# The last block of an MLP: partial sums loaded by plain transfers and added by VectorE

## The chip, the cores and the metric

One Trainium2 chip; the program runs on one of its cores. The metric is the device time of one execution in microseconds (us), as the median of several executions. The engines are called by the profile's names: PE (TensorE matmul) with its weight loads PEld, DVE (VectorE), ACT (ScalarE), POOL (GpSimd) and SP (SyncE). POOL and SP hardly compute here; they issue DMA transfers, POOL on queue q0, SP on queue q1. Both queues are served by the same 16 DMA engines.

## The reference

A decoder of two layers on 256 tokens of width 2048, in float32. Each layer is an attention mixer, an MLP and a gated embedding; the two mixers differ, the two MLPs don't. What matters here is the MLP:

```python
D_MODEL, SEQ, DEPTH = 2048, 256, 2
D_FF = 4 * D_MODEL
...
    for i in range(DEPTH):
        ...                                       # mixer A (i = 0) or mixer B (i = 1)
        hn = rmsnorm(h, mlp_norm_g[i])
        h = h + jnp.square(jax.nn.relu(hn @ mlp_w1[i])) @ mlp_w2[i]
        gate = jax.nn.sigmoid(rmsnorm(h, ple_norm_g[i]) @ ple_w_gate[i])
        h = h + (p[i] @ ple_w_proj[i]) * gate
    return rmsnorm(h, final_norm_g)
```

## The kernel before, in words

**Products.** A float32 product is made of three matmuls: each operand is split into a rounded part and a rest. A weight chunk is 128x1024 (512 KB). SP loads it into `raw` (L240, 5 buffers), ACT writes its rounded part `whi` (L252, 6 buffers), DVE the rest `wlo` (L260, 5 buffers); PE multiplies by both. An ordinary chunk is twelve matmuls, four of them with `wlo`. `Program.run` writes out the order of all this: when it emits the matmuls of a chunk it has emitted the splits of the three chunks behind it, and every generator that is under way (an epilogue, a fetch) goes on by one `yield` a chunk. There is no scheduler beyond that: each engine runs its instructions in the order in which they were emitted, and waits for semaphores. An instruction that waits on DVE therefore holds up every `wlo` behind it.

**The MLP** (`mlp`, L738). The hidden width of 8192 goes in four blocks b = 0 to 3 of 2048; each block has four column quarters q of 512, in w1 (up) and in w2 (down). The down results of all blocks have to be summed: for b < 3, `down_kept` (L902) puts each quarter's result through POOL into the DRAM tiles `y[q]`, with an adding transfer where b > 0 (`keep_sum`, L846). The last block adds those sums to its own results, turns each 128x1024 row tile to the layout of the residual x (`turned`, L698: DVE transposes it, one transfer takes it to DRAM, four bring it back) and adds it to x (`add_turned`, L726).

**Pairs of quarters.** Quarters 0 and 1 of a down block are made together (`pair_major`, L470). For some chunks it makes seven products in place of eight (a scheme of Strassen's kind), four of them into PSUM banks of their own: P1, R6, Q5, Q7. These are kept apart, summed over the blocks in DRAM as `shared[q]` (two tiles, in the profile `s`), and only at the end combined by four 128x512 operations of DVE (`from_sums`, L881, operations L882 to L885) and added to both quarters. In blocks 0 to 2 quarters 2 and 3 are a pair too; in the last block they are made one after the other by `downs`, and need the kept sums `shared[2]` and `y[2]`, `y[3]` alone.

**The last block, b = 3.** Around `down_mixed(3, 0)`, the pair (0, 1), 18 chunks, numbered 0 to 17 here, and then two times eight chunks of `downs(3, 2)` and `downs(3, 3)`:

- `down_last` (L920). After the chunks of the four extra products, ACT copies P1 and R6 into one row tile and Q5 and Q7 into another (L928), POOL adds the kept `shared[0]` to each by an adding transfer (L930), DVE combines (`from_sums`), POOL adds `y[0]` and `y[1]` by adding transfers (L936). Then `done` adds the pair's own banks, quarter 0 after chunk 15 and quarter 1 after chunk 17 (L945), and starts the turning.
- `fetch(2)` (L887), begun after chunk 14: POOL loads `shared[2]` into two row tiles (L890), DVE combines, POOL adds `y[2]`, `y[3]` (L896). `down` uses these tiles (L856).
- Ahead of all this the last two up quarters of the block pass through POOL: `dU<-z`, four `w<-dU` and four `y<-dU` (L206, L210), each ending in a tile `h` that ACT and DVE split (L778, L780). The first `h` is read from chunk 10 on, the second from chunk 14 on.

Row tiles have the tag `y` (4 buffers, L976). The tag `xf` has four 128x1024 tiles: sums of activations that the up products of the pairs read (`x_forms`, L557); after the last `up_mixed` of a layer nothing reads them.

Of the kernel before, what the change touches and what calls it, by code (L numbers as in the profile page):

```python
# [11 lines left out]
F32R = mybir.dt.float32r  # L12
AF = mybir.ActivationFunctionType
ALU = mybir.AluOpType

P = 128
D = 2048
T = 256
# [10 lines left out]
NFB = 4  # L29
# [8 lines left out]
MIXED = (2, 3, 5, 6)  # L38
# [10 lines left out]
def mixed_down(b, q):  # L49
    return (0, 4) if (b, q) not in ((0, 0), (NFB - 1, 0)) else (0,)  # L50


def f32(ap):
    return ap.bitcast(F32)
# [116 lines left out]
def kernel(ctx: ExitStack, tc: tile.TileContext, a: dict, out: bass.AP):  # L171
    nc = tc.nc
# [12 lines left out]
    cur = {}  # L185
# [535 lines left out]
    def add_turned(q, w):  # L721

        for n in range(2):
            xn = xp[2 * q + n].rearrange("p (f a r) -> p f a r", a=4, r=32)
            wn = w.rearrange("p a (f r) -> p f a r", r=32)[:, 4 * n:4 * n + 4]
            nc.vector.tensor_add(xn, wn, xn)  # L726

    def in_pairs(make, q):

        for n in (0, 2):  # L730
            gs = [make(4 * q + n + i) for i in range(2)]
            for g in gs:
                next(g)
            yield
            for g in gs:
                next(g, None)

    def mlp(layer, xg, norm, to, norm2, opening):  # L738
# [6 lines left out]
        y = [dpool.tile([P, D // 2], F32, tag=f"y{q}", name=f"y{q}", bufs=1) for q in range(4)]  # L745
        shared = {q: [dpool.tile([P, D // 2], F32, tag=f"s{q}{i}", name=f"s{q}{i}", bufs=1) for i in range(2)] for q in (0, 2)}
        hid = [[None] * 16 for _ in range(NFB)]
        forms = [None] * (KT // 2)
        sums_so_far = {}
# [5 lines left out]
        def row():  # L755
            return row_tile()
# [118 lines left out]
        def all_forms(these):  # L875
            for c in these:
                yield from x_forms(2 * c, G_MLP + layer, forms)
                yield
        taken_late(lambda: ups(0, 0, {4: [lambda: norm.factor(rows=True)]}), lambda: ups(0, 1), opening,
                   [lambda: all_forms(MIXED[:3])])  # L880
        def from_sums(r, o):  # L881
            nc.vector.tensor_sub(r[:, 1], r[:, 1], r[:, 0])  # L882
            nc.vector.tensor_add(o[:, 0], o[:, 0], r[:, 1])
            nc.vector.tensor_sub(r[:, 1], o[:, 1], r[:, 1])
            nc.vector.tensor_sub(o[:, 1], o[:, 0], o[:, 1])  # L885

        def fetch(q):  # L887
            rows = row(), row()
            for i in range(2):
                nc.gpsimd.dma_start(flat(rows[i]), shared[q][i])  # L890
            for _ in range(4):
                yield
            from_sums(*rows)
            yield
            for i in range(2):
                nc.gpsimd.dma_start(flat(rows[i]), y[q + i], accum_op=ALU.add)  # L896
                sums_so_far[q + i] = rows[i]

        def turning_tile(n):
            return f32(cur["z"].tile([P, 2, 2 * T], F32R, tag="hf", name="hf", bufs=2).rearrange("p c n -> p (c n)"))  # L900
# [20 lines left out]
        def down_last(q):  # L921
            ts = []

            def sums(aux):
                rows = row(), row()
                for t, names, kept in zip(rows, (("P1", "R6"), ("Q5", "Q7")), shared[q]):
                    for j, n in enumerate(names):
                        nc.scalar.copy(t[:, j], aux[n])  # L928
                    yield
                    nc.gpsimd.dma_start(flat(t), kept, accum_op=ALU.add)  # L930
                for _ in range(4):
                    yield
                from_sums(*rows)
                yield
                for i in range(2):
                    nc.gpsimd.dma_start(flat(rows[i]), y[q + i], accum_op=ALU.add)  # L936
                for _ in range(2):
                    yield
                ts.extend(rows)

            def done(i, ps):
                while not ts:
                    yield
                t = ts[i]
                nc.vector.tensor_add(t, ps, t)  # L945
                yield
                w = yield from turned(t, turning_tile if i else new, steps=3)
                add_turned(q + i, w)
                yield
                yield from in_pairs(normed, q + i)  # L950

            return sums, done

        def down_mixed(b, q):
            sums, done = down_kept(b, q) if b < NFB - 1 else down_last(q)
            m = mixed_down(b, q)
            if (b, q) == (0, 0):
                order = [(i, c) for i in range(2) for c in (1, 2, 3)] + [(0,)] + [(i, c) for c in (4, 5) for i in range(2)]
            else:
                order = [(0, c) for c in (1, 2, 3)] + [(0,)] + [(1, c) for c in (1, 2, 3)]  # L960
                order += [(0, 5), (1, 5), (4,)] if len(m) == 2 else [(i, c) for c in (4, 5) for i in range(2)]
            order += [(i, c) for i in range(2) for c in (6, 7)]
            pair_major(lambda i, c: a["w2"][layer * 128 + (b * 4 + q + i) * 8 + c], order, hid[b], turned_forms[b], sums, done,
                       {(0, 0): {13: [lambda: all_forms(MIXED[3:])]}, (NFB - 1, 0): {14: [lambda: fetch(2)]}}.get((b, q)), (3, 1, 0, 2))

        up_mixed(0, 2)
        for b in range(NFB):
# [11 lines left out]
    def flat(t):  # L979
        return t.rearrange("p j c -> p (j c)")  # L980

    def row_tile():

        return cur["h"].tile([P, 2, 512], F32, tag="y", name="y", bufs=4)
# [1017 lines left out]
```

## Time and profile before

| | |
|---|---|
| runs | 2425.81, 2426.03, 2428.92 us; median 2426.03 us |
| profiled execution | 2427.97 us; its span from first to last instruction 2426.2 us |
| granted TensorE clock over the span | 0.998 |
| PE, PEld busy | 99%, 83% of the span |
| DVE, ACT, POOL busy | 82%, 61%, 6% of the span |
| HBM | 504.39 MB read, 59.24 MB written |

The times are of whole executions, the rows of the profile of one of them; 1.8 us lie around its span. The MLP's last block stands twice in the trace, in layer 0 at about 1060 to 1150 us and in layer 1 at about 2225 to 2315 us. In a timeline row the columns are the start, the duration, the engine, the line, the operation with its tiles, how many were merged, and in brackets the idle time of the engine ahead of it with what ended it. A busy PE is not PE at its peak, but an idle gap of PE is time that the program waits.

### The profile page before, as it was taken

Reading aid. Unit: us, or ns where it says so; the run is one execution under the profiler, and the core shown is the slowest. Engines: PE = TensorE matmul, PEld = TensorE weight load, DVE = VectorE, ACT = ScalarE, POOL = GpSimd, SP = SyncE. Lnnn points to the kernel's source line nnn. Section 1 sums busy time; section 2 is a strip of 40 time slices with the busy share of each in tenths; the row PEclk is TensorE's granted clock in tenths of the full one; section 3 lists DMA queues with packets and bytes.
Section 4 is the critical chain, followed back from the end, with each engine's and each line's share of the span. In section 5 each row is a group of like instructions: output and inputs, shape, how many; then the busy total and the mean of one; then the engine's idle time right before and its main releaser. Section 6 shows DMA issues by size and latency. Waiting matters only on the chain.

```text
span 2426.2 us, 33519 instructions
## 1 busy us (share of the span) xinstructions
PE 2405.9 (99%) x11613; PEld 2023.3 (83%) x11613; DVE 1987.6 (82%) x2960; ACT 1480.0 (61%) x2161; POOL 147.6 (6%) x246
## 2 busy tenths in 40 slices
PE   9999999999999999999999999999999999999998
PEld 8888888888888888887788889988888888888787
DVE  7867687688898988886777989867898898888676
ACT  6544444567566666664664788756666666666456
POOL 0000000001001100111000000000100100111000
PEclk9999999999999999999999999999999999999999
DMA  8666666778778788879886753476777878888985
GB/s 282 204 216 213 199 208 193 223 216 270 245 248 260 247 255 258 249 250 284 257 247 209 256 176 120 131 226 218 254 239 260 260 252 252 258 246 259 286 254 151
DMA packets 171882, 565.85 MB, mean 233 GB/s; under 512 B 20608, under 2 KB 36416, under 8 KB 171712
## 3 DMA queue, kind: packets, MB, share of 16 engines
q1 hardware_dynamic: 150672, 494.73, 63.4%
q0 software_dynamic: 20464, 68.19, 11.0%
q8 instruction: 91, 1.49, 0.3%
q10 hardware_dynamic: 576, 0.79, 0.1%
q14 instruction: 79, 0.65, 0.1%
HBM read 504.39 MB, written 59.24 MB: 232 GB/s over the span
## 4 chain that ended last, share of the span: by engine, by line
PE 90%; issue 4%; DMA 4%; DVE 1%; POOL 0%; ACT 0%; SPq 0%; ACTq 0%; DVEq 0%; POOLq 0%
PE at L502 33%; PE at L598 13%; PE mm L393 11%; PE mm L598 11%; PE mm L502 8%; PE mm L395 6%; PE at L393 1%; DMA dU<-z 1%; DMA y<-s 1%; DMA raw<-in_w 1%; PE at L395 1%; DVE wlo L260 1%; PE at L1824 1%; DMA w<-dU 0%; PE mm L1848 0%
## 5 line engine op out<-in xcount | busy, mean ns | idle before, releaser
L260 DVE TENSOR_TENSOR wlo<-raw,whi 128x1024 fp32r<-128x1024 f32 (+1 forms) x953 | 1094.9, 1171 | 252.7 <-ACT whi L252 85.0
L252 ACT CAST whi<-raw 128x1024 fp32r<-128x1024 f32 (+1 forms) x953 | 939.2, 1013 | 451.8 <-DMA raw<-in_w 133.4
L502 PE MATMUL at<-whi,h 128*128 128x512 f32 x1504 | 463.3, 389 | 0.4 <-DVE h L780 0.4
L393 PE MATMUL mm<-xa,whi 128*128 128x512 f32 x1104 | 372.4, 396 | 0.0
L502 PE MATMUL at<-whi,xa 128*128 128x512 f32 x1144 | 352.1, 389 | 0.0
L502 PEld LDWEIGHTS at<-whi,h 128*128 128x128 f32 x1504 | 282.3, 188 | 59.5 <-DVE h L780 0.8
L502 PE MATMUL at<-wlo,h 128*128 128x512 f32 x752 | 292.7, 389 | 0.4 <-DVE wlo L260 0.4
L395 PE MATMUL mm<-xa,wlo 128*128 128x256 f32 x1104 | 274.2, 278 | 0.0
L502 PEld LDWEIGHTS at<-whi,xa 128*128 128x128 f32 x1144 | 214.7, 188 | 44.5
L502 PE MATMUL at<-wlo,xa 128*128 128x512 f32 x572 | 222.5, 389 | 0.0
L395 PEld LDWEIGHTS mm<-xa,wlo 128*128 128x128 f32 x1104 | 207.3, 188 | 17.7
L393 PEld LDWEIGHTS mm<-xa,whi 128*128 128x128 f32 x1104 | 193.5, 188 | 31.0 <-issue 0.4
L598 PE MATMUL at<-whi,xa 128*128 128x512 f32 x672 | 208.1, 391 | 0.1
L598 PE MATMUL mm<-whi,xa 128*128 128x512 f32 x656 | 202.7, 390 | 0.0
L502 PEld LDWEIGHTS at<-wlo,h 128*128 128x128 f32 x752 | 141.1, 188 | 30.0 <-DVE wlo L260 0.8
L252 ACT CAST whi<-ts 128x1024 fp32r<-128x1024 f32 x78 | 82.0, 1051 | 123.0 <-DVE ts L540 122.1
L598 PEld LDWEIGHTS at<-whi,xa 128*128 128x128 f32 x672 | 124.8, 188 | 26.3 <-ACT whi L252 0.8
L598 PEld LDWEIGHTS mm<-whi,xa 128*128 128x128 f32 x656 | 122.5, 188 | 25.0
L598 PE MATMUL at<-wlo,xa 128*128 128x512 f32 x336 | 130.9, 391 | 0.2 <-DVE wlo L260 0.2
L598 PE MATMUL mm<-wlo,xa 128*128 128x512 f32 x328 | 127.7, 389 | 0.0
L502 PEld LDWEIGHTS at<-wlo,xa 128*128 128x128 f32 x572 | 107.4, 188 | 22.4
L260 DVE TENSOR_TENSOR wlo<-ts,whi 128x1024 fp32r<-128x1024 f32 x78 | 95.1, 1220 | 8.8 <-PE at L502 4.5
(445 smaller groups left out, 3377.9 us busy)
## 6 DMA issues: line engine op xcount, KB each, us to landing
raw<-in_w SPq DMA_DIRECT2D x512, 512.0 KB, 5.2
raw<-in_w_qk SPq DMA_DIRECT2D x96, 512.0 KB, 4.2
raw<-in_w_gate SPq DMA_DIRECT2D x64, 512.0 KB, 4.8
raw<-in_w_kv SPq DMA_DIRECT2D x48, 512.0 KB, 4.4
raw<-in_w_v SPq DMA_DIRECT2D x47, 512.0 KB, 4.5
y<-y POOLq DMA_DIRECT2D x32, 512.0 KB, 9.2
raw<-in_w_q SPq DMA_DIRECT2D x32, 512.0 KB, 4.4
raw<-in_w_oB SPq DMA_DIRECT2D x32, 512.0 KB, 3.7
```

What stands on the lines that cost most here:

```text
L252: nc.scalar.copy(hi[:, c], t[:, c])
L260: nc.vector.tensor_sub(lo[:, c], t[:, c], f32(hi)[:, c])
L393: nc.tensor.matmul(ps, hi[:, col:col + P], rhs, start=first, stop=False)
L395: nc.tensor.matmul(ps[:, :T], lo[:, col:col + P], rhs[:, :T], start=False, stop=last)
L502: nc.tensor.matmul(ps, x_, w_, start=b not in touched, stop=end and last[b] == n and i == 2)
L598: nc.tensor.matmul(st[j], *parts[j][i], start=k == i == 0, stop=k == kt - 1 and i == 2)
L1824: nc.tensor.transpose(tr[:, i * P:(i + 1) * P], src, ident)
```

## The change

Nothing adds by transfer in the last block any more. `fetch_shared(q)` loads the two kept product sums `shared[q]` by plain transfers into two `xf` tiles, `fetch(q)` loads `y[q]` into a row tile. `down_last` lets DVE add the PSUM banks to the loaded tiles (four adds of 128x512, in place of ACT's four copies), then `from_sums`, then DVE adds the row tiles (`with_y`, 128x1024 each). `finish_sums(2)` does the same for quarters 2 and 3, with two more adds. The loads are hooks: `shared[0]` after chunk 1, `y[0]` and `y[1]` after chunk 6, `shared[2]` after chunk 12, `y[2]` and `y[3]` after chunk 14.

```diff
--- before.py
+++ after.py
@@ -884,17 +884,31 @@
             nc.vector.tensor_sub(r[:, 1], o[:, 1], r[:, 1])
             nc.vector.tensor_sub(o[:, 1], o[:, 0], o[:, 1])
 
+        kept = {}
+
+        def fetch_shared(q):
+
+            kept[q] = [cur["z"].tile([P, 2, 2 * T], F32R, tag="xf", name="xf", bufs=len(MIXED)) for _ in range(2)]
+            kept[q] = [f32(t) for t in kept[q]]
+            for i in range(2):
+                nc.gpsimd.dma_start(kept[q][i], shared[q][i])
+
         def fetch(q):
-            rows = row(), row()
+            sums_so_far[q] = row()
+            nc.gpsimd.dma_start(flat(sums_so_far[q]), y[q])
+
+        def with_y(q, i):
+            nc.vector.tensor_add(kept[q][i], kept[q][i], sums_so_far[q + i])
+            sums_so_far[q + i] = kept[q][i]
+
+        def finish_sums(q):
+            for _ in range(6):
+                yield
+            from_sums(*kept[q])
             for i in range(2):
-                nc.gpsimd.dma_start(flat(rows[i]), shared[q][i])
-            for _ in range(4):
-                yield
-            from_sums(*rows)
-            yield
-            for i in range(2):
-                nc.gpsimd.dma_start(flat(rows[i]), y[q + i], accum_op=ALU.add)
-                sums_so_far[q + i] = rows[i]
+                for _ in range(2):
+                    yield
+                with_y(q, i)
 
         def turning_tile(n):
             return f32(cur["z"].tile([P, 2, 2 * T], F32R, tag="hf", name="hf", bufs=2).rearrange("p c n -> p (c n)"))
@@ -922,21 +936,17 @@
             ts = []
 
             def sums(aux):
-                rows = row(), row()
-                for t, names, kept in zip(rows, (("P1", "R6"), ("Q5", "Q7")), shared[q]):
+                for _ in range(3):
+                    yield
+                for t, names in zip(kept[q], (("P1", "R6"), ("Q5", "Q7"))):
                     for j, n in enumerate(names):
-                        nc.scalar.copy(t[:, j], aux[n])
+                        nc.vector.tensor_add(t[:, j], aux[n], t[:, j])
                     yield
-                    nc.gpsimd.dma_start(flat(t), kept, accum_op=ALU.add)
-                for _ in range(4):
+                from_sums(*kept[q])
+                for i in range(2):
                     yield
-                from_sums(*rows)
-                yield
-                for i in range(2):
-                    nc.gpsimd.dma_start(flat(rows[i]), y[q + i], accum_op=ALU.add)
-                for _ in range(2):
-                    yield
-                ts.extend(rows)
+                    with_y(q, i)
+                ts.extend(kept[q])
 
             def done(i, ps):
                 while not ts:
@@ -961,7 +971,9 @@
                 order += [(0, 5), (1, 5), (4,)] if len(m) == 2 else [(i, c) for c in (4, 5) for i in range(2)]
             order += [(i, c) for i in range(2) for c in (6, 7)]
             pair_major(lambda i, c: a["w2"][layer * 128 + (b * 4 + q + i) * 8 + c], order, hid[b], turned_forms[b], sums, done,
-                       {(0, 0): {13: [lambda: all_forms(MIXED[3:])]}, (NFB - 1, 0): {14: [lambda: fetch(2)]}}.get((b, q)), (3, 1, 0, 2))
+                       {(0, 0): {13: [lambda: all_forms(MIXED[3:])]}, (NFB - 1, 0): {1: [lambda: fetch_shared(0)], 6: [lambda: fetch(0), lambda: fetch(1)],
+                                         12: [lambda: fetch_shared(2)],
+                                         14: [lambda: fetch(2), lambda: fetch(3), lambda: finish_sums(2)]}}.get((b, q)), (3, 1, 0, 2))
 
         up_mixed(0, 2)
         for b in range(NFB):
```

PE has the same instructions in the same order. ACT loses the four copies. On DVE and POOL the order is another; layer 1 is shown, layer 0 has the same.

POOL before, from the turning of the last two up quarters to the end of the block (`s00`, `s01`, `s20`, `s21` are the kept products, `y0` to `y3` at the right of an arrow the kept results):

```order
L206 DMA dU_20578<-z_20557 128x1024
L210 DMA w_20577<-dU_20578 32x4x256 x4
L206 DMA dU_20664<-z_20645 128x1024
L210 DMA y_20663<-dU_20664 32x4x256 x4
L930 DMA y_20709<-s00_109 128x1024
L930 DMA y_20710<-s01_110 128x1024
L936 DMA y_20709<-y0_105 128x1024
L936 DMA y_20710<-y1_106 128x1024
L890 DMA y_20864<-s20_111 128x1024
L890 DMA y_20865<-s21_112 128x1024
L896 DMA y_20864<-y2_107 128x1024
L896 DMA y_20865<-y3_108 128x1024
```

POOL now, the same stretch:

```order
L206 DMA dU_20586<-z_20565 128x1024
L894 DMA xf_20625<-s00_109 128x1024
L894 DMA xf_20626<-s01_110 128x1024
L210 DMA w_20585<-dU_20586 32x4x256 x4
L206 DMA dU_20676<-z_20657 128x1024
L210 DMA y_20675<-dU_20676 32x4x256 x4
L898 DMA y_20714<-y0_105 128x1024
L898 DMA y_20716<-y1_106 128x1024
L894 DMA xf_20838<-s20_111 128x1024
L894 DMA xf_20839<-s21_112 128x1024
L898 DMA y_20880<-y2_107 128x1024
L898 DMA y_20882<-y3_108 128x1024
```

There are eight transfers of 512 KB as before; two of them have moved ahead of `w<-dU`, and none of the eight waits for a result of `from_sums` any more (before, the rows of L936 and L896 did).

DVE before, between the two splits of `h` and the first combination (`mm` and `at` are PSUM banks):

```order
L780 TENSOR_TENSOR h<-w,h 128x4x8x32
L260 TENSOR_TENSOR wlo<-raw,whi 128x1024 x5
L780 TENSOR_TENSOR h<-y,h 128x4x8x32
L260 TENSOR_TENSOR wlo<-raw,whi 128x1024
L882 TENSOR_TENSOR y<-y 128x512
L883 TENSOR_TENSOR y<-y 128x512
L884 TENSOR_TENSOR y<-y 128x512
L885 TENSOR_TENSOR y<-y 128x512
L260 TENSOR_TENSOR wlo<-raw,whi 128x1024 x3
L945 TENSOR_TENSOR y<-at,y 128x1024
```

DVE now, the same place:

```order
L943 TENSOR_TENSOR xf<-mm,xf 128x512 x2
L260 TENSOR_TENSOR wlo<-raw,whi 128x1024
L780 TENSOR_TENSOR h<-y,h 128x4x8x32
L882 TENSOR_TENSOR xf<-xf 128x512
L883 TENSOR_TENSOR xf<-xf 128x512
L884 TENSOR_TENSOR xf<-xf 128x512
L885 TENSOR_TENSOR xf<-xf 128x512
L260 TENSOR_TENSOR wlo<-raw,whi 128x1024
L901 TENSOR_TENSOR xf<-xf,y 128x1024
L260 TENSOR_TENSOR wlo<-raw,whi 128x1024
L901 TENSOR_TENSOR xf<-xf,y 128x1024
L260 TENSOR_TENSOR wlo<-raw,whi 128x1024 x2
```

The operations of L943 and L901 are new: four of the one (the first two stand a split ahead of these rows) and two of the other come before quarter 0's own sum, which was L945, is L955 now and stands right behind these rows. The combination stands one split earlier.

DVE before, from the turning of quarter 0 to that of quarter 1:

```order
L709 STREAM_TRANSPOSE z<-y 128x2x4x4x32
L260 TENSOR_TENSOR wlo<-raw,whi 128x1024
L882 TENSOR_TENSOR y<-y 128x512
L883 TENSOR_TENSOR y<-y 128x512
L884 TENSOR_TENSOR y<-y 128x512
L885 TENSOR_TENSOR y<-y 128x512
L945 TENSOR_TENSOR y<-at,y 128x1024
L260 TENSOR_TENSOR wlo<-raw,whi 128x1024
L709 STREAM_TRANSPOSE hf<-y 128x2x4x4x32
```

DVE now, the same stretch and what follows it:

```order
L709 STREAM_TRANSPOSE z<-xf 128x2x4x4x32
L260 TENSOR_TENSOR wlo<-raw,whi 128x1024
L955 TENSOR_TENSOR xf<-at,xf 128x1024
L260 TENSOR_TENSOR wlo<-raw,whi 128x1024
L709 STREAM_TRANSPOSE hf<-xf 128x2x4x4x32
L260 TENSOR_TENSOR wlo<-raw,whi 128x1024
L882 TENSOR_TENSOR xf<-xf 128x512
L883 TENSOR_TENSOR xf<-xf 128x512
L884 TENSOR_TENSOR xf<-xf 128x512
L885 TENSOR_TENSOR xf<-xf 128x512
L260 TENSOR_TENSOR wlo<-raw,whi 128x1024 x2
L901 TENSOR_TENSOR xf<-xf,y 128x1024
```

The combination for quarters 2 and 3 has moved behind quarter 1's sum and its turning, with two splits between.

## The prediction

> **What bounds the kernel now.** I read the page first, then the idle gaps of PE in both last blocks, then what stood ahead of the late instruction on its engine, then the transfers.
>
> ```profile
> PE 2405.9 (99%) x11613; PEld 2023.3 (83%) x11613; DVE 1987.6 (82%) x2960; ACT 1480.0 (61%) x2161; POOL 147.6 (6%) x246
> ```
>
> PE is busy for 2405.9 us of the span of 2426.2 us. Nothing can be won from its work, which the change leaves alone; what can be won is idle time of PE. The timeline of PE has these gaps in the two last blocks, and no others:
>
> ```profile
> 1113.37 0.61 PE L598 MATMUL mm<-whi,h 128*128 128x512 f32 x2
> 1116.72 0.50 PE L598 MATMUL mm<-wlo,h 128*128 128x512 f32 x1 [2.73 <-DVE wlo L260]
> ...
> 1140.03 0.50 PE L598 MATMUL at<-wlo,h 128*128 128x512 f32 x1 [1.21 <-DVE wlo L260]
> ...
> 1143.75 0.50 PE L598 MATMUL at<-wlo,h 128*128 128x512 f32 x1 [0.70 <-DVE wlo L260]
> ...
> 1183.88 0.61 PE L298 MATMUL mm<-ones,acc 128*128 128x1 f32 x4 [1.93 <-DVE acc L289]
> ...
> 2277.38 0.61 PE L598 MATMUL mm<-whi,h 128*128 128x512 f32 x2
> 2281.24 0.50 PE L598 MATMUL mm<-wlo,h 128*128 128x512 f32 x1 [3.25 <-DVE wlo L260]
> ...
> 2282.29 1.05 PE L598 MATMUL mm<-whi,h 128*128 128x512 f32 x2
> ```
>
> The two large ones, 2.73 us in layer 0 and 3.25 us in layer 1, stand at the same place, the fifth chunk of `downs(3, 2)`, and end with a late `wlo`. Behind the second, two matmuls take 1.05 us in place of 0.61 us. Why that `wlo` is late shows in DVE's timeline, layer 1:
>
> ```profile
> 2254.65 0.68 DVE L882 TENSOR_TENSOR y<-y 128x512 f32<-128x512 f32 x1
> 2258.16 0.69 DVE L883 TENSOR_TENSOR y<-y 128x512 f32<-128x512 f32 x1 [2.82 <-DMA y<-s]
> ...
> 2260.22 3.49 DVE L260 TENSOR_TENSOR wlo<-raw,whi 128x1024 fp32r<-128x1024 f32 x3
> 2265.39 1.23 DVE L945 TENSOR_TENSOR y<-at,y 128x1024 f32<-128x1024 f32 x1 [1.69 <-DMA y<-y]
> ...
> 2272.95 0.69 DVE L882 TENSOR_TENSOR y<-y 128x512 f32<-128x512 f32 x1 [2.94 <-DMA y<-s]
> 2276.78 0.69 DVE L883 TENSOR_TENSOR y<-y 128x512 f32<-128x512 f32 x1 [3.13 <-DMA y<-s]
> ...
> 2278.84 1.22 DVE L945 TENSOR_TENSOR y<-at,y 128x1024 f32<-128x1024 f32 x1
> 2279.97 1.21 DVE L260 TENSOR_TENSOR wlo<-raw,whi 128x1024 fp32r<-128x1024 f32 x1
> ```
>
> DVE waits four times for POOL's transfers, 2.82 + 1.69 + 2.94 + 3.13 = 10.6 us, all ahead of the `wlo` at 2279.97. The waits of DVE in layer 0, from 1080 to 1120 us, are the same ones:
>
> ```profile
> DVE y L883 <- DMA y<-s: 5.1, 2, 3.2
> ...
> DVE y L882 <- DMA y<-s: 2.0, 1, 2.0
> DVE y L945 <- DMA y<-y: 1.6, 1, 1.6
> ```
>
> Together 8.7 us. The loads come late because they stand in a chain, as POOL's timeline shows:
>
> ```profile
> 2243.33 0.99 POOL L930 DMA_DIRECT2D y<-s  x1
> 2245.19 0.89 POOL L930 DMA_DIRECT2D y<-s  x1 [0.86 <-ACT y L928]
> 2259.87 1.74 POOL L936 DMA_DIRECT2D y<-y  x2 [13.79 <-DVE y L884]
> 2261.13 1.58 POOL L890 DMA_DIRECT2D y<-s  x2
> 2278.49 1.80 POOL L896 DMA_DIRECT2D y<-y  x2 [15.79 <-DVE y L884]
> ```
>
> Adding transfer, DVE, adding transfer: POOL waits 13.79 and 15.79 us for `from_sums`, and `s20`, `s21` (L890), which need nothing but a place, queue behind the first wait.
>
> **The change part by part.** DVE's waits go. The kept `s00`, `s01` now go out right behind the first `dU<-z`, long before DVE adds to them; `y0`, `y1`, `s20`, `s21` and `y2` follow `y<-dU` without waiting for `from_sums`. What DVE gets for it, per layer: four adds from PSUM and four of 128x1024, and ACT loses four copies.
>
> ```profile
> L812 DVE TENSOR_TENSOR y<-mm,y x14: 682/683/686, 554.9 to 2216.3; 128x512 f32<-128x512 f32 x14
> ...
> L928 ACT COPY y<-mm x8: 577/584/592, 1077.5 to 2244.3; 128x512 f32<-128x512 f32 x8
> ```
>
> An add from PSUM is 0.68 us (L812 has the same shape), one of 128x1024 is 1.22 us (L945 above): 4 x 0.68 + 4 x 1.22 = 7.6 us more on DVE, 4 x 0.58 = 2.3 us less on ACT, which is not late here and gets no credit. Ahead of the late `wlo` stand only the four small adds and two of the large, 2.7 + 2.4 = 5.2 us, while the second `from_sums`, 4 x 0.69 = 2.8 us, moves behind it. So, even with no add hidden, that `wlo` comes 10.6 + 2.8 - 5.2 = 8.2 us earlier in layer 1 and 8.7 + 2.8 - 5.2 = 6.3 us in layer 0. PE needs 3.25 and 2.73 us of that. **Both gaps go, with 4.9 and 3.6 us to spare: 3.25 + 2.73 = 6.0 us.** What is late next is the chunk's `raw`, which waits for the buffer that `wlo` frees and so moves with it.
>
> The gaps of 1.21 and 0.70 us in layer 0 come from DVE too. It is held up just ahead of them by the turned quarter 1:
>
> ```profile
> 1136.35 1.29 DVE L726 TENSOR_TENSOR x<-hf,x 128x512 f32<-128x512 f32 x2 [1.18 <-DMA hf<-dU]
> ```
>
> That quarter's turning begins some 6 us earlier (the `wlo` behind its sum does), PE only 2.7 us. The gaps shrink by up to 1.9 us; none is possible if the loads then collide with the turning. Layer 1, with the same code, has no such gap, so I take 1.4 us. The gap of 1.93 us ends the MLP: the norm of the last quarter, whose turning waits behind the earlier ones on DVE. Between 0 and 1.9 us I take 1.0 us, the middle, since layer 1 has no gap there.
>
> The clock. These are four rows of busy time by stage (columns: length, PE, PEld, DVE, ACT, POOL, granted clock, share of the DMA engines, GB/s):
>
> ```profile
> 1060.00:1080.00 20.00, 19.61 (x86) 15.79 (x86) 18.04 (x17) 13.45 (x17) 5.04 (x10) 1.00 0.75 250
> 1080.00:1100.00 20.00, 20.00 (x90) 16.53 (x89) 11.97 (x12) 11.19 (x13) 4.85 (x7) 1.00 0.94 269
> ...
> 2240.00:2260.00 20.00, 20.00 (x90) 16.57 (x89) 11.64 (x12) 9.72 (x11) 4.19 (x7) 1.00 1.01 312
> ...
> 2280.00:2300.00 20.00, 18.76 (x76) 15.33 (x77) 14.19 (x18) 8.30 (x14) 0.29 (x1) 0.91 1.03 285
> ```
>
> Behind the gap of 3.25 us the clock is 0.91 over 20 us, which costs 0.09 x 20 = 1.8 us; behind that of 2.73 us none is lost. The loss goes with the gap. The profiled execution, 2427.97 us, is 1.94 us over the median of 2426.03 us, about this loss; I take it that the median execution lacks it and credit it against the profiled one alone. [...]
>
> The loads' price. Queue totals of the page, and the landing of the loads from POOL:
>
> ```profile
> q1 hardware_dynamic: 150672, 494.73, 63.4%
> q0 software_dynamic: 20464, 68.19, 11.0%
> ...
> y<-s POOLq DMA_DIRECT2D x8, 512.0 KB, 12.3
> ```
>
> On q1, where all is plain, 63.4% of 2426.2 us for 494.73 MB is 3.11 us a MB, 1.63 us of all engines for 512 KB. On q0 it is 266.9 us for 68.19 MB, 55 us more than at that price; over its 44 adding transfers (32 of the earlier blocks, 12 here) that is up to 1.25 us each, an estimate. Six of the eight loads of a layer lose it, 7.5 us of DMA time where the share is 0.94 to 1.03. That gets no credit of its own, but is why I expect `raw` no later.
>
> What may cost: `s00` and `s01`, 2 x 1.63 = 3.3 us, now run ahead of `w<-dU`, and so of the second `h`.
>
> ```profile
> 1089.42 1.23 DVE L780 TENSOR_TENSOR h<-y,h 128x1024 fp32r<-128x1024 f32 x1 [3.20 <-ACT h L778]
> ...
> 1091.61 0.61 PE L502 MATMUL at<-whi,h 128*128 128x512 f32 x2
> ...
> 2251.81 1.23 DVE L780 TENSOR_TENSOR h<-y,h 128x1024 fp32r<-128x1024 f32 x1 [0.20 <-ACT h L778]
> ...
> 2255.61 0.62 PE L502 MATMUL at<-whi,h 128*128 128x512 f32 x2
> ```
>
> The PE rows are the starts of chunk 14, the first to read that `h`. Ready at 1090.65 and 2253.04, it has 0.96 and 2.57 us to spare. Bounds: no wait, or 3.3 us less the spare, 2.3 + 0.7 = 3.0 us. The loads fall in a stretch with a DMA share of 0.75, 5 us free of 20, so nearer to none: 0.5 us, in layer 0.
>
> **Sum.** 3.25 + 2.73 + 1.4 + 1.0 - 0.5 = 7.9 us; with the clock 9.7 us against the profiled execution, 2427.97 - 9.7 = 2418.3 us; against the median 2426.03 - 7.9 = 2418.1 us. I predict 2418.2 us.
>
> **The rivals.**
>
> *The burst starves `raw`* (no change). Five loads queue at once on q0, where two did: 5 x 1.63 = 8.2 us of all engines. If q0 and q1 take turns, that lasts 16.3 us, in which q1 gets 8.2 us, five chunks. PE's pace is in the chain:
>
> ```profile
> 2293.58 21.76 PE at L598 x96
> ```
>
> Eight chunks in 21.76 us, 2.72 us each, six in 16.3 us. One chunk late, 2.7 us, is less than the 3.6 us to spare; with the turnings on top two may be, 5.4 us. Then PE waits 1.8 and 0.5 us again and the smaller gaps stay: 7.9 - 2.3 - 2.4 = 3.2 us won, 2422.8 us. For it: the share of 1.01. Against: the 7.5 us of DMA time that fall away. [...]
>
> *DVE becomes the bound.* 7.6 us of adds against 8.7 to 10.6 us of waits: if what is left goes into the turnings, the smaller gaps stay and only the large ones go, 6.0 - 0.5 = 5.5 us, 2420.5 us. Against: DVE is busy for 11.97 and 11.64 of 20 us there.
>
> *The turned `h` is late* (slower). If `w<-dU`, the second `dU<-z` and `y<-dU`, each behind the other, all lose the 3.3 us of the two loads, the second `h` is 9.8 us late; PE waits 8.8 and 7.2 us at chunk 14 and loses the clock twice, 1.8 us each: 19.6 - 7.9 = 11.7 us slower, 2437.7 us. It decides from d with (d - 0.96) + (d - 2.57) + 3.6 = 7.9, 3.9 us of delay. Against: only `w<-dU` is directly behind the loads.
>
> *Nothing starts earlier* (no change): POOL held at an `xf` tile that PE still reads, 2426 us. Against: `xf` is read by up products alone, and POOL's order has the loads behind the turning of those products' results.
>
> **How the numbers follow.** Forecast 0.70; DVE as the bound 0.09; starved `raw` 0.13; late `h` 0.05; nothing earlier 0.03. The low end has all gaps whole, 2.73 + 1.91 + 1.93 + 3.25 = 9.8 us, and the clock in the median too, 1.8 us: 2414.4, say 2414.2 us. The high end takes in starved `raw`: 2423.0 us. 0.2%, about what a measurement can tell, is 4.9 us, so faster means under 2421.2 us: 0.68 of the forecast and 0.07 of DVE's case, 0.75; slower 0.05; the rest 0.20.
>
> **What would show it.** Right: no wait of DVE for a transfer ahead of `from_sums` or the quarters' sums; no gap of PE at the fifth chunk of `downs(3, 2)`; a clock of 1.00 there; POOL's loads with no wait for DVE, but for `y3`, whose place the second `h` frees. Wrong: a gap of PE ahead of `at<-whi,h` at chunk 14 (late `h`), ACT waiting for `raw` with PE idle (the burst), or `wlo` late with DVE busy all along.

## The result, and the profile after

| | before | after |
|---|---|---|
| median of the runs | 2425.98 us (2425.81 to 2428.92, 4 runs) | 2414.42 us (2414.18 to 2414.48, 4 runs) |
| profiled execution, span | 2427.97, 2426.2 us | 2414.44, 2412.7 us |

The ratio is 0.9949, 95% interval 0.9932 to 0.9967: 11.6 us faster by the medians, where 7.8 us were predicted. The range began at 2414.2 us: the median is just inside it, and by the ratio, 0.9949 x 2426.03 = 2413.7 us, the time is just below. PE's work is the same 11613 matmuls; the page of the changed kernel has

```profile
PE 2402.0 (100%) x11613; PEld 2023.0 (84%) x11613; DVE 2001.4 (83%) x2976; ACT 1477.6 (61%) x2153; POOL 142.6 (6%) x246
...
q1 hardware_dynamic: 150672, 494.73, 63.9%
q0 software_dynamic: 20464, 68.19, 10.5%
```

Packets and MB of both queues are the same as before; q0 takes 253.3 us of all 16 engines in place of 266.9 (share times span), 13.6 us less for twelve transfers that no longer add, 1.1 us each. These are PE's rows in the changed kernel at the places of the former gaps:

```profile
1113.31 0.39 PE L598 MATMUL mm<-wlo,h 128*128 128x512 f32 x1
...
1135.07 0.39 PE L598 MATMUL at<-wlo,h 128*128 128x512 f32 x1
...
1137.79 0.39 PE L598 MATMUL at<-wlo,h 128*128 128x512 f32 x1
...
1175.42 0.50 PE L298 MATMUL mm<-ones,acc 128*128 128x1 f32 x4
...
2269.56 0.39 PE L598 MATMUL mm<-wlo,h 128*128 128x512 f32 x1
```

No row carries a wait any more. Taken from the starts of the same five matmuls before, they stand 3.41, 4.96, 5.96, 8.46 and 11.68 us earlier. Of the first figure 0.38 us arose ahead of the place, at a gap of 0.39 us (a `wlo`, at 1072.89 us before) that the prediction's list lacks. So the five places are worth 3.03, 1.55, 1.00, 2.50 and 3.22 us, and by the `wlo` matmul at 2285.69 before another 1.73 us of half clock (granted 0.50 from 2283 to 2285 us in before) are gone. That makes 13.4 of the 13.5 us between the two profiled executions.

Where DVE waited for transfers for 10.6 us in layer 1, its timeline now has:

```profile
2246.74 0.68 DVE L882 TENSOR_TENSOR xf<-xf 128x512 f32<-128x512 f32 x1
2247.46 0.69 DVE L883 TENSOR_TENSOR xf<-xf 128x512 f32<-128x512 f32 x1
...
2250.66 1.22 DVE L901 TENSOR_TENSOR xf<-xf,y 128x1024 f32<-128x1024 f32 x1
...
2256.34 1.22 DVE L955 TENSOR_TENSOR xf<-at,xf 128x1024 f32<-128x1024 f32 x1
...
2260.87 1.21 DVE L955 TENSOR_TENSOR xf<-at,xf 128x1024 f32<-128x1024 f32 x1
2262.00 1.21 DVE L260 TENSOR_TENSOR wlo<-raw,whi 128x1024 fp32r<-128x1024 f32 x1
```

The `wlo` that was late starts at 2262.00 in place of 2279.97 us. Of these 18.0 us PE had won 8.5 in layer 0; 9.5 us are layer 1's own, where the prediction had 8.2. The chain that ends the MLP in layer 0 now reads, from the transposition of quarter 1's sum to the last turned rows (the norm's matmul is the row at 1175.42 above):

```profile
1106.55 1.24 DVE L709 STREAM_TRANSPOSE hf<-xf 128x1024 f32<-128x1024 f32 x1
...
1124.13 1.29 DVE L726 TENSOR_TENSOR x<-hf,x 128x512 f32<-128x512 f32 x2 [0.50 <-DMA hf<-dU]
1125.34 1.28 DVE L856 TENSOR_TENSOR xf<-mm,xf 128x512 f32<-128x512 f32 x2
...
1129.13 1.24 DVE L709 STREAM_TRANSPOSE z<-xf 128x1024 f32<-128x1024 f32 x1
...
1142.99 1.29 DVE L726 TENSOR_TENSOR x<-w,x 128x512 f32<-128x512 f32 x2 [4.05 <-DMA w<-dU]
...
1147.94 1.28 DVE L856 TENSOR_TENSOR xf<-at,xf 128x512 f32<-128x512 f32 x2
...
1151.73 1.24 DVE L709 STREAM_TRANSPOSE z<-xf 128x1024 f32<-128x1024 f32 x1
...
1164.27 1.29 DVE L726 TENSOR_TENSOR x<-w,x 128x512 f32<-128x512 f32 x2 [3.69 <-DMA w<-dU]
```

Quarter 1's turned rows (L726, `x<-hf`) stand on DVE ahead of quarter 2's sum (L856), this one ahead of quarter 2's turning, that one ahead of quarter 3's sum, and so to the norm. Before, the row `x<-hf` stood at 1136.35 and the norm's matmul, waiting, at 1183.88 us: 47.5 us. After, it is 51.3 us and PE does not wait, so the chain has some 3.8 us to spare. In before the transposition (DVE's timeline) was at

```profile
1116.58 1.24 DVE L709 STREAM_TRANSPOSE hf<-y 128x1024 f32<-128x1024 f32 x1
```

so quarter 1's sum comes 10.0 us earlier, and its turning, L709 to L726, takes 17.6 us in place of 19.8. Together 12.2 us. In layer 1 the turning is no shorter: 17.5 us before (2281.11 to 2298.58), 17.9 after (2263.13 to 2281.07).

### The profile page after: what moved, and what is told of

It reads as the page before. It is cut to its first block, busy times and chain, and to the rows that moved or that the text cites. A ratio compares the mean times of both kernels' runs of the same rounds, so it can differ in the third digit from the quotient of the medians.

```text
span 2412.7 us, 33516 instructions
## 1 busy us (share of the span) xinstructions
PE 2402.0 (100%) x11613; PEld 2023.0 (84%) x11613; DVE 2001.4 (83%) x2976; ACT 1477.6 (61%) x2153; POOL 142.6 (6%) x246
## 3 DMA queue, kind: packets, MB, share of 16 engines
q0 software_dynamic: 20464, 68.19, 10.5%
## 4 chain that ended last, share of the span: by engine, by line
PE 99%; DMA 0%; ACT 0%; DVE 0%; issue 0%; SPq 0%; ACTq 0%; DVEq 0%
PE at L502 39%; PE at L598 14%; PE mm L598 13%; PE mm L393 11%; PE mm L502 9%; PE mm L395 6%; PE at L393 1%; PE at L395 1%; PE at L1836 1%; PE mm L1860 0%; PE mm L1599 0%; PE mm L1600 0%; PE mm L1066 0%; PE mm L1068 0%; PE mm L1067 0%; DMA raw<-in_w_v 0%
## 5 line engine op out<-in xcount | busy, mean ns | idle before, releaser
L395 PEld LDWEIGHTS mm<-xa,wlo 128*128 128x128 f32 x1104 | 207.4, 188 | 17.6
## 6 DMA issues: line engine op xcount, KB each, us to landing
y<-y POOLq DMA_DIRECT2D x32, 512.0 KB, 10.7
```

The costliest lines, as they stand in the source:

```text
L395: nc.tensor.matmul(ps[:, :T], lo[:, col:col + P], rhs[:, :T], start=False, stop=last)
```

## The experiments

Three theories stood at the start. *Order*: DVE, whose rows stand in the order of the program (the late `wlo`, at 2279.97, right behind the sum at 2278.84), waited for POOL's chained loads; with the waits gone all is gained. *Price*: an adding transfer takes more of the DMA engines than a plain one. *Copies*: ACT is relieved of four copies a layer. Two more came from the first runs: *collision* (a transfer costs where it runs beside quarter 1's turning) and *chain* (the MLP ends a fixed time behind that turning). Each group of four ran on one chip, beside the kernel before, whose median was 2426.1, 2426.6 and 2426.2 us there; its single runs spread from 2421.0 to 2433.1 us.

**The kernel before again.**

> The kernel before once more, unchanged, with a second profile. [...] The gaps of 2.73, 1.21, 0.70, 1.93 and 3.25 us should be there again within 0.3 us; what moves more is noise of the runs.

2424.5 us. The gaps were not the same. In layer 0: 0.49 us at the fifth chunk of `downs(3, 2)` (2.73 expected), 1.60 and 0.69 us for the pair, 0.69 us at the norm (1.93 expected). In layer 1: 1.93 us at the fifth chunk (3.25 expected), and 0.30 and 2.14 us at later places where the first execution had none. No clock was lost behind the 1.93 us (busy time by stage):

```profile
2280.00:2300.00 20.00, 20.00 (x90) 16.57 (x89) 13.82 (x20) 10.46 (x19) 0.00 (x0) 1.00 1.02 311
```

The gaps change by up to 2.2 us from one execution to the next, and the lower clock behind the fifth chunk of layer 1 (0.91 over 20 us in the first execution) is not in this one; a single run can't say how often it comes. It agrees with crediting the clock against the profiled execution alone.

**Order alone.** In the kernel before, `fetch` (L887) waits two steps longer:

```diff
-            for _ in range(4):
+            for _ in range(6):
                 yield
             from_sums(*rows)
```

> The kernel before with all its adding transfers and its copies on ACT; only the second from_sums is put two steps later, so that it stands on VectorE behind the sum of quarter 1 and the wlo that was late. Theory 'order' (VectorE waits in program order for POOL's chained loads ahead of that wlo): two of the four waits (2.94 + 3.13 us in layer 1, 2.0 + 1.9 us in layer 0) and the four subtractions (2.8 us) no longer stand ahead of it; it comes 8.9 and 6.7 us earlier, the gaps of 3.25 and 2.73 us go, quarter 1 turns earlier by the same and the later gaps go for the most part: 2415 to 2419 us. Theory 'price' (the gain comes from transfers that no longer add): all twelve still add, 2426 us. Theory 'copies' (ACT is relieved of four copies a layer): 2426 us.

2424.7 us, ratio 0.9992, 95% interval 0.9982 to 1.0001: the theory fails as to the time. PE's rows show why:

```profile
1136.99 0.50 PE L598 MATMUL at<-wlo,h 128*128 128x512 f32 x1 [1.78 <-DVE wlo L260]
...
1181.32 0.61 PE L298 MATMUL mm<-ones,acc 128*128 128x1 f32 x4 [2.07 <-DVE acc L289]
...
2300.03 0.50 PE L598 MATMUL at<-wlo,h 128*128 128x512 f32 x1 [1.69 <-DVE wlo L260]
...
2344.28 0.61 PE L298 MATMUL mm<-ones,acc 128*128 128x1 f32 x4 [2.56 <-DVE acc L289]
```

The two large gaps are gone, as expected. But the time comes back as later gaps, because quarter 1's turning got long (DVE's timeline):

```profile
1107.87 1.24 DVE L709 STREAM_TRANSPOSE hf<-y 128x1024 f32<-128x1024 f32 x1
...
1133.31 1.29 DVE L726 TENSOR_TENSOR x<-hf,x 128x512 f32<-128x512 f32 x2 [1.42 <-DMA hf<-dU]
```

25.4 us against 19.8 before. The adding transfers of `y2` and `y3`, issued from 1112.8 us on and 8.3 and 10.9 us under way, now fall between the turning's way to DRAM (issued at 1109.1) and its way back; in before they were issued at 1114.0, ahead of both. The turning's five transfers landed after 10.2 us by the median, in place of 7.3. The norm is 48.0 us behind `x<-hf`; in before it was 47.5.

**One pair of quarters alone.** First quarters 0 and 1 in the new form, with the old `fetch(2)` for 2 and 3; then the other way round.

```diff
-                                         12: [lambda: fetch_shared(2)],
-                                         14: [lambda: fetch(2), lambda: fetch(3), lambda: finish_sums(2)]}
+                                         14: [lambda: fetch_adding(2)]}    # the fetch of before
```

> The change for quarters 0 and 1 alone: their kept sums and y come by plain loads, VectorE adds; quarters 2 and 3 keep the old chain (load, from_sums, adding transfer), at its old place. Theory 'order': the waits of 2.82 and 1.69 us go, and POOL, which no longer waits 13.8 us for the first from_sums, issues the loads for quarters 2 and 3 so early that the second from_sums finds them landed; its 2.8 us still stand ahead of the wlo. That wlo comes some 8 us earlier: 2414.5 to 2417 us. Theory 'price': half of the transfers no longer add, half of the gain, 2420 us. Theory 'copies': all four copies a layer are gone, 2414.4 us.

2423.9 us, ratio 0.9982, 95% interval 0.9969 to 0.9994. No theory gave this time: POOL's second load of a kept sum waited 9.1 us for a row tile, and the adding transfers of `y2`, `y3` were issued at 1107.0 us, beside the turning, which took 22.4 us (1109.61 to 1132.06). All four copies a layer are off ACT here and 2.2 us are won, so *copies* is out as the main cause.

```diff
-{1: [lambda: fetch_shared(0)], 6: [lambda: fetch(0), lambda: fetch(1)],
-                                         12: [lambda: fetch_shared(2)],
+{12: [lambda: fetch_shared(2)],
...
         def down_last(q):      # sums() is that of before, with copies and adding transfers
```

> The change for quarters 2 and 3 alone: their loads are plain and early and their from_sums stands behind the late wlo; quarters 0 and 1 keep the copies on ACT and the chain of adding transfers, whose waits (2.82 + 1.69 us in layer 1, 3.2 + 1.6 us in layer 0) stay. Theory 'order': the waits of 2.94 + 3.13 and 2.0 + 1.9 us and the four subtractions of 2.8 us no longer stand ahead of the wlo, 8.9 and 6.7 us: both large gaps go, 2415 to 2419 us. If VectorE still waits for the first chain longer than before, because four more loads run beside it, some of the later gaps stay. Theory 'price': half of the gain, 2420 us. Theory 'copies': 2426 us.

2420.1 us, ratio 0.9967, 95% interval 0.9955 to 0.9979. Both large gaps go; the turning takes 19.9 us (1109.32 to 1129.25), and PE waits for the norm 1.9 and 1.4 us (and 0.22 and 0.69 us ahead of it in layer 1). Half of the gain, as *price* had it, but with the copies still on ACT. Order and price change together in this run; the runs of all eight transfers, below, part them.

**The changed kernel again.**

> The changed kernel once more, unchanged, beside the kernel before on one chip. The executions of before spread over 12 us on the last chip, with mean clocks of 0.997 to 0.999. If that spread comes of gaps of PE (some long enough for the half clock behind them), the changed kernel, whose PE has no gap in the two last blocks, has none: 2414.2 to 2414.8 us each time, and 11 to 12 us less than the median of before. If the spread is the chip's, it is there too.

2416.1 us (2415.1 to 2416.5) against 2426.6, ratio 0.9954, 95% interval 0.9942 to 0.9966: 10.6 us less, a little under the 11 to 12 expected, and a little over the expected times. On this chip seventeen executions of before spread over 9.5 us, five of the changed kernel over 1.4. That the spread comes of PE's gaps is not shown: the last run below, whose profile has no gap in the two last blocks either, spread over 6.4 us in six executions.

**All eight transfers adding, at the new places.** POOL fills each tile with zeros first, then adds:

```diff
+                nc.gpsimd.memset(kept[q][i], 0.0)
-                nc.gpsimd.dma_start(kept[q][i], shared[q][i])
+                nc.gpsimd.dma_start(kept[q][i], shared[q][i], accum_op=ALU.add)
...
+            nc.gpsimd.memset(sums_so_far[q], 0.0)
-            nc.gpsimd.dma_start(flat(sums_so_far[q]), y[q])
+            nc.gpsimd.dma_start(flat(sums_so_far[q]), y[q], accum_op=ALU.add)
```

> The changed kernel, but POOL fills each of the eight tiles of a layer with zeros and the transfer adds to them: the same places, the same order on VectorE and ACT, and all eight transfers at the adding price, no fewer than before. Theory 'order': the loads are early enough whatever they cost, 2414.5 to 2416 us. Theory 'price' (an adding transfer takes up to 1.25 us more of all DMA engines, 10 us a layer, and that makes the raw chunks or the turning late): most of the gain is gone, 2420 to 2426 us. Theory 'collision' (an adding transfer costs where it runs beside quarter 1's turning, which took 25.4 us with the second from_sums moved and 17.6 us in the changed kernel): the eight land before 1110 us, ahead of most of that turning, which becomes no more than 2 us longer: 2414.5 to 2417 us.

2426.7 us, ratio 0.9999, 95% interval 0.9988 to 1.0010: nothing is left of the gain, a little worse than *price* had it. The control, the same fills with plain transfers:

> The run in which all eight transfers of a layer add, with the same fills of zeros on POOL ahead of each, but plain transfers: what the fills cost by themselves (each holds POOL's next issue back by 1.0 to 1.9 us, 5 us at the eighth). Theory 'price' (the adding transfers fill the DMA engines, make raw late and with it quarter 1's sum): with plain ones the gaps stay away, 2414.5 to 2417 us, and quarter 1 is turned by 1126 us in layer 0 as in the changed kernel (1124.1), not at 1134.6 us. Theory 'fills' (POOL's later issues lost the gain there): 2422 to 2427 us again.

2415.8 us, ratio 0.9953, 95% interval 0.9939 to 0.9967 (in the third group): the fills cost nothing that can be measured, and the adding form costs 11.0 us. What it costs the DMA engines, from 1080 to 1110 us, all adding:

```profile
DMA packets 2276, 8.16 MB, mean 272 GB/s; under 512 B 286, under 2 KB 286, under 8 KB 2275
...
q1 hardware_dynamic: 1387, 5.05, 52.4%
q0 software_dynamic: 888, 3.10, 52.3%
...
raw<-in_w SPq DMA_DIRECT2D x10, 512.0 KB, 12.4
```

and all plain, with the fills:

```profile
DMA packets 3085, 11.08 MB, mean 369 GB/s; under 512 B 384, under 2 KB 384, under 8 KB 3084
...
q1 hardware_dynamic: 2031, 7.40, 68.5%
q0 software_dynamic: 1053, 3.66, 33.5%
...
raw<-in_w SPq DMA_DIRECT2D x12, 512.0 KB, 6.8
```

The columns of a queue are packets, MB, and share of 16 engines. On q0 that is 0.523 x 480 / 3.10 = 81 us of engine time a MB with adding, 0.335 x 480 / 3.66 = 44 without; q1 stands at 50 and 44. So a load of 512 KB takes 2.65 us of all engines when it adds and 1.44 when it doesn't, 1.2 us more. (In both stretches about 0.5 MB on q0 are the plain `y<-dU`, so 2.65 is rather low.) With the engines full in both runs (q0 and q1 together 104.7% and 102.0%), q1 gets 2.35 MB less, four to five chunks in 30 us, and a `raw` lands 12.4 us after its issue in place of 6.8.

How the queues share shows where they fill the engines, 105.4% and 102.2% together. All adding, 1092 to 1112 us:

```profile
q0 software_dynamic: 751, 2.75, 68.9%
q1 hardware_dynamic: 750, 2.74, 36.5%
```

and the changed kernel, 1084 to 1100 us:

```profile
q0 software_dynamic: 878, 3.17, 53.5%
q1 hardware_dynamic: 797, 2.92, 48.7%
```

In both the queues move about the same number of packets, so with adding q0 takes 1.9 times the time of q1 for the same bytes (68.9% and 36.5%). PE takes a chunk in 2.72 us (the prediction's row), 5.9 in 16 us and 7.4 in 20 us. Beside plain loads q1 brings 2.92 MB, 5.6 chunks in the 16 us; beside adding ones 2.74 MB, 5.2 chunks in the 20 us. The first shortage is small enough to be hidden, the second isn't. In the run of all adding DVE's rows are

```profile
1093.03 1.23 DVE L780 TENSOR_TENSOR h<-y,h 128x1024 fp32r<-128x1024 f32 x1 [3.83 <-ACT h L778]
...
1106.14 1.23 DVE L260 TENSOR_TENSOR wlo<-raw,whi 128x1024 fp32r<-128x1024 f32 x1 [1.15 <-ACT whi L252]
...
1109.96 1.23 DVE L260 TENSOR_TENSOR wlo<-raw,whi 128x1024 fp32r<-128x1024 f32 x1 [1.44 <-ACT whi L252]
...
1113.75 1.23 DVE L260 TENSOR_TENSOR wlo<-raw,whi 128x1024 fp32r<-128x1024 f32 x1 [1.43 <-ACT whi L252]
```

Two things are late. The second `h` is split 5.2 us later than in the control (1087.84 there), and PE waits 0.92 and 0.77 us at chunk 14. Then the splits stand 3.8 us apart, as `raw` comes, where PE wants one in 2.72; the waits for ACT, which in turn waits mostly for `raw`, add 4.0 us, and the control has none at these places. (ACT's total wait for `raw` does not tell the runs apart: from 1080 to 1120 us it is 13.5 us here, 12.1 in the changed kernel.) Quarter 1's sum is transposed at 1114.89 us, 9.5 us later than in the control, and its rows are turned at 1134.60, 10.5 us later than in the changed kernel; the norm follows 48.0 us behind, at 1182.58 us.

**y of quarters 2 and 3 late.** Issued behind the second `from_sums`, by adding transfers and by plain ones:

```diff
             from_sums(*kept[q])
             for i in range(2):
-                for _ in range(2):
-                    yield
-                with_y(q, i)
+                nc.gpsimd.dma_start(kept[q][i].rearrange("p j c -> p (j c)"), y[q + i], accum_op=ALU.add)
+                sums_so_far[q + i] = kept[q][i]
...
-                                         14: [lambda: fetch(2), lambda: fetch(3), lambda: finish_sums(2)]}}.get((b, q)), (3, 1, 0, 2))
+                                         14: [lambda: finish_sums(2)]}}.get((b, q)), (3, 1, 0, 2))
```

> The changed kernel with y of quarters 2 and 3 alone added by the old adding transfers, issued behind the second from_sums, some 1112 us in layer 0, beside the turning of quarters 0 and 1. All that stands ahead of the late wlo on VectorE is as in the changed kernel. Theory 'order': no gap comes back, 2414.5 us. Theory 'collision': quarter 1's turning takes 22 to 26 us in place of 17.6, and as quarter 2's sum, its turning, quarter 3's sum, its turning and the norm follow it one by one, the spare of some 3.4 us there is used up and PE waits for the last norm and ahead of it: 2417 to 2422 us.

```diff
             from_sums(*kept[q])
             for i in range(2):
-                for _ in range(2):
-                    yield
+                sums_so_far[q + i] = row()
+                nc.vector.tensor_add(sums_so_far[q + i][:, 0, :256], kept[q][1][:, 0, :256], kept[q][1][:, 1, :256])
+                nc.gpsimd.dma_start(flat(sums_so_far[q + i]), y[q + i])
+            for _ in range(2):
+                yield
+            for i in range(2):
+                yield
                 with_y(q, i)
...
```

> As the one before, with y of quarters 2 and 3 late at the same place (two small additions on VectorE into their tiles hold them back until from_sums is done), but by plain loads, and added on VectorE. Theory 'order': 2414.5 us. Theory 'collision, by bytes': a plain load beside the turning costs it nearly as much as an adding one, 2417 to 2421 us. Theory 'collision, by price': the adding one costs about twice the plain one, so half of the loss: the turning takes 19.5 to 21.5 us, 2415 to 2417.5 us.

2418.0 us (ratio 0.9961, 95% interval 0.9949 to 0.9974) and 2417.7 us (0.9961, 0.9949 to 0.9973). By the medians both lose 1.5 to 2 us against the changed kernel on that chip, though the intervals overlap. The rows of the adding one show it at the chain:

```profile
1109.08 1.24 DVE L709 STREAM_TRANSPOSE hf<-xf 128x1024 f32<-128x1024 f32 x1
...
1132.85 1.29 DVE L726 TENSOR_TENSOR x<-hf,x 128x512 f32<-128x512 f32 x2 [3.95 <-DMA hf<-dU]
```

23.8 us; with plain loads 22.6 us (1107.94 to 1130.59), in place of 17.6 to 18.3 in layer 0 of three profiles with the loads early (the changed kernel twice, and the control). In layer 1 it is 22.6 and 22.4 us, in place of 17.9 to 20.3. So in either form the two late loads cost some 5 us in layer 0 and less in layer 1. That it is the bytes alone which count, *collision, by bytes*, is not shown, because DVE waits differently in the two. With plain loads the turned rows wait for no transfer; DVE itself waits for `y2` and `y3`, 4.01 and 1.20 us, ahead of them:

```profile
1121.29 1.23 DVE L901 TENSOR_TENSOR xf<-xf,y 128x1024 f32<-128x1024 f32 x1 [4.01 <-DMA y<-y]
...
1124.85 1.23 DVE L901 TENSOR_TENSOR xf<-xf,y 128x1024 f32<-128x1024 f32 x1 [1.20 <-DMA y<-y]
...
1130.59 1.29 DVE L726 TENSOR_TENSOR x<-hf,x 128x512 f32<-128x512 f32 x2
```

With adding ones DVE waits 3.95 us for the turning's own transfers, as its second row above shows. By the median these five transfers land after 13.3 us beside the adding loads, 10.7 beside the plain ones and 7.3 in the changed kernel. So there is a collision, and the adding form costs more of it, but in the plain form DVE's own waits bring the rows nearly to the same place.

**VectorE later, no transfer changed.** In `with_y`, y of quarters 0 and 1 is taken off and put on again k times (k = 2, 1):

```diff
             nc.vector.tensor_add(kept[q][i], kept[q][i], sums_so_far[q + i])
+            for _ in range(k if q == 0 else 0):
+                nc.vector.tensor_sub(kept[q][i], kept[q][i], sums_so_far[q + i])
+                nc.vector.tensor_add(kept[q][i], kept[q][i], sums_so_far[q + i])
```

> The changed kernel with eight more additions of 128x1024 on VectorE a layer (y of quarters 0 and 1 taken off and put on again twice), ahead of the sum of quarter 0: 8 x 1.13 = 9.1 us of VectorE's time and no transfer changed. Theory 'chain' (from quarter 1's turned rows on, at 1124.1 us in layer 0, the adds, turnings and the norm follow one another and end some 47.5 us later; the changed kernel's PE needs the norm 51.3 and 50.6 us later, so 3.8 and 3.1 us are to spare): quarter 1 is 9.1 us later, PE waits 5.3 and 6.0 us a layer by the norm, of it some 2.4 us already at the wlo that was late (6.5 us to spare there): 2425 to 2428 us. Theory 'transfers' (only the DMA engines matter): VectorE is busy for 83% of the span and takes it up, 2414.5 to 2416 us.

> The same with four more additions a layer, 4.5 us. Theory 'chain': no gap at the wlo (6.5 us to spare), the norm late by 4.5 - 3.8 = 0.7 us in layer 0 and 4.5 - 3.1 = 1.4 us in layer 1: 2415.5 to 2418 us. If it is 2423 us or more, something ahead of the chain has less to spare than I read.

2432.9 us (ratio 1.0025, 95% interval 1.0015 to 1.0034) and 2420.8 us (0.9977, 0.9965 to 0.9988): more than was reckoned for the chain, both over their ranges. PE waited at a `wlo` that I had not counted, ahead of quarter 0's turning. With four more additions:

```profile
1104.00 0.50 PE L598 MATMUL mm<-wlo,h 128*128 128x512 f32 x1 [1.54 <-DVE wlo L260]
```

and with eight:

```profile
1109.51 0.80 PE L598 MATMUL mm<-wlo,h 128*128 128x512 f32 x1 [4.29 <-DVE wlo L260]
```

With eight, the lower clock adds to it (granted 0.91 from 1100 to 1120 us): behind the gaps of 4.29 us in both layers two `whi` matmuls take 1.05 us in place of 0.62, and PE takes 3.05 us for the 7 matmuls from 1109.51 and 5.57 us for the 13 from 2274.40. At the pace of 12 in 2.72 us that is 1.5 + 2.6 = 4.1 us lost beside the gaps. The additions stand 1.25 us apart, not 1.13 as reckoned (DVE's timeline, eight more):

```profile
1094.75 1.22 DVE L901 TENSOR_TENSOR xf<-xf,y 128x1024 f32<-128x1024 f32 x1
1096.01 1.22 DVE L903 TENSOR_TENSOR xf<-xf,y 128x1024 f32<-128x1024 f32 x1
```

So the changed kernel has some 3.5 us to spare at this `wlo` in layer 0 (5.0 less 1.5), less than the 6.5 counted at the later one. The chain held: where PE waited for the norm, it came 48.7 and 47.3 us (four) and 48.3 us (eight, layer 0) behind `x<-hf`.

**The second `from_sums` back ahead of the wlo.**

```diff
         def finish_sums(q):
-            for _ in range(6):
+            for _ in range(4):
                 yield
             from_sums(*kept[q])
```

> The changed kernel with the second from_sums put back ahead of quarter 1's sum and of the wlo that was late, where it stood before; its loads are plain and have landed by then. The prediction counted its 2.8 us as part of what the wlo gains. Theory 'chain': the wlo has 6.5 us to spare and quarter 1's turned rows 3.8 and 3.1 us, so 2.8 us later changes nothing: 2414.4 to 2415.5 us. Theory 'order': the place of that from_sums is what matters, 2417 to 2420 us.

2415.3 us, ratio 0.9954, 95% interval 0.9939 to 0.9968: the ratio that the changed kernel had in the second group. Its place is worth nothing that can be measured once the loads have landed.

## Why the prediction was right and wrong

**Right.** The large gaps of 3.25 and 2.73 us go and measure 3.22 and 3.03 us; DVE waits for no transfer ahead of the sums; POOL's loads don't wait for DVE but for `y3` (5.65 and 5.58 us). No version of the experiments has a lower median than the changed kernel, and with no gap of PE left in the two last blocks a shorter wait there has nothing more to give.

**Wrong: the later gaps, taken as halves and each by itself.** The steps of the sum that failed are "so I take 1.4 us", which measured 2.55, and "I take 1.0 us, the middle", which measured 2.50. With the -0.5 us for a late second `h`, where nothing was lost, that is 3.2 of the 3.8 us by which the 9.7 us against the profiled execution fell short of 13.5. Another 0.4 us is the gap at 1072.89, which the second execution of before doesn't have either, so it may be no merit of the change. The reason for the halves was that layer 1 has no gap at these places; the second execution of before has 0.30 and 2.14 us there, so their lack was that of one execution.

What the runs showed in place of separate gaps is one chain. The run of order alone took the two large gaps away and was 1.4 us faster, if at all: PE came earlier to a chain that had not moved as far. The norm comes some 46 to 49 us behind quarter 1's turned rows in every profile where PE waited for it, in both layers, so what counts is when these rows are there. They came 12.2 us earlier in layer 0, where the prediction had "some 6 us" for the start of the turning. Of the 5.9 us of difference, 2.2 are the shorter turning, which it did not price, and which layer 1 does not show. 3.7 us are quarter 1's sum, 10.0 in place of 6.3 us earlier: the four adds from PSUM, 2.7 us, run where DVE waits for the second `h` anyway, and were counted as if nothing hid them; 1.0 us I can't assign. PE needs 8.46 us of the 12.2 by the norm, hence whole gaps where halves were taken. The low end of the range had all gaps whole and the clock too, and there the time fell.

**Undersold: the loads' price.** Of 7.5 us of DMA time a layer the prediction said "That gets no credit of its own, but is why I expect `raw` no later". The estimate was good (up to 1.25 us more for an adding load; 1.2 measured in the burst, 1.1 by the queue totals), and the use made of it was right. What it did not say is that the whole forecast stands on it: with the same places and the same order on DVE, adding transfers give 2426.7 us and plain ones 2415.8. Early loads are only harmless here because they are cheap, 1.44 us of all engines for 512 KB in place of 2.65. *The burst starves raw* and *the turned h is late* were therefore no idle rivals: with adding loads both came true together. With plain ones the turns that the first supposed came too, for some 16 us (878 packets on q0 and 797 on q1), but left q1 less than one chunk short, which the prediction had rightly reckoned to be within the spare. That the queues take turns was a supposition; with adding loads the counts fit it, 751 packets on q0 and 750 on q1 in 20 us, and q0's took 1.9 times as long.

**DVE as the bound** did not come true, but was not far: the changed kernel's DVE is busy for 19.90 of 20 us from 1100 to 1120 us with no gap of PE, and four more additions a layer (5.0 us in each) cost about 5 us in all.

**What stays open.** Whether plain loads in the old chain, with DVE waiting for them, would win a part: that corner was not tried.

## What to carry to other kernels

A gap of PE can be the shadow of one chain; taking away the wait that shows then only moves PE up to the chain's next link (order alone took gaps of 2.73 and 3.25 us away and won 1.4 us, if anything), so ask how far the whole chain moves, to its end. When the DMA engines are full, price a transfer in engine time a byte, by form: one that adds took 1.8 to 1.9 times a plain one here, and who paid was the weight stream beside it: q1 moved as many packets as q0 (750 and 751 in 20 us), but a `raw` landed 12.4 us after its issue in place of 6.8. The early loads were free only while they were cheap (2415.8 us with plain ones, 2426.7 with adding ones) and landed before something urgent needed the queues; two late loads beside a turning cost it up to some 5 us in either form, through the queues and, where DVE has to add them, through DVE's order. And a gap that one profile lacks may be there in the next execution (0.30 and 2.14 us in the second of before).

## What was not expected of the hardware

The lower clock followed short gaps as well as long ones. In the run of order alone it followed the gap of 1.78 us at 1136.99 (busy time by stage, granted clock in the third column from the right):

```profile
1120.00:1140.00 20.00, 18.22 (x76) 14.67 (x75) 11.47 (x18) 10.08 (x20) 2.60 (x6) 0.94 0.93 265
```

In the run of quarters 2 and 3 alone it followed one of 1.45 us (0.95 and 0.97 in the two stretches of 20 us from 2320 on), whereas the gaps of 2.73 us (before) and 1.93 us (before again) cost none. So the length of a gap does not tell here whether the clock falls behind it, and what does tell is not shown. Such an event cost 1.73 us in the profiled execution; what else is in the 9.5 to 12 us over which before spreads stays open.
